# Attention's queries and keys projected token-major, in seven block products for eight, with the residual parked in DRAM

## The chip, the cores and the metric

One core of one Trainium2 chip runs the whole kernel. The metric is the device time in microseconds (us) of one execution. The profile and the trace are of one execution of the same program on the chip.

## The reference, cut to what matters

The program is a two-layer decoder trunk over 256 positions of width 2048, in float32. Layer 0 mixes by two recurrences, layer 1 by attention; each is followed by an MLP of width 8192. The change lies in layer 1's attention.

```python
qkv = (h @ w_qkv).astype(F32).reshape(bsz, seq, 3, ATTN_HEADS, HEAD_DIM)   # 16 heads of 128
q = partial_rope(qkv[:, :, 0], positions) * (HEAD_DIM ** -0.5)             # first 32 of 128 columns
k = partial_rope(qkv[:, :, 1], positions)
v = qkv[:, :, 2]
branches = [dilated_branch(q, k, v, w, d) for (w, d) in DILATED_GROUPS]    # (128,1) (512,4) (2048,16)
...                                                                        # merged by their softmax denominators
out = (num / den).reshape(bsz, seq, D_MODEL).astype(h.dtype)
return out @ w_o
```

`h` is `rms_norm(x, gain)`: the reciprocal root of each token's mean square multiplies whole rows, so it can be applied after a product with weights as well as before it.

## The kernel before, in words

**Number format.** Every float32 operand of a large product is split into a rounded part `hi` and a rest `lo`; a product is three TensorE products (hi*hi, hi*lo, lo*hi). Weights arrive as "units", tiles of 128x2048, one 1 MB DMA each on SP's queue, in one fixed order (the list `units`, filled ahead of the program). `unit()` hands out the next one and lets `fetch()` prepare the one that is two or three further on. `Weights.split` makes `hi` on ScalarE (L104) and `lo` on VectorE (L105); three buffers each for raw, hi and lo.

**Two ways to project.** *Feature-major* (`project`, with `cross`): a block of 128 output columns is the stationary operand's width, the 256 tokens stream; one unit is one block of 128 columns over all 16 blocks of the contraction, by 16 matmuls of 512 columns (hi of the weights against hi and lo of the tokens side by side) and 16 of 256 columns (lo of the weights). The result has features on partitions. *Token-major in pairs* (`blocks`): 8 units are 1024 output columns. Their first eight contraction blocks (the order `PAIRED`) are cut into 2 x 2 x 2 sub-blocks (even and odd contraction blocks, two halves of the tokens `j`, two groups of 512 columns `n`), and seven block products, three of them of sums of weights and sums of tokens (`formx`), replace eight; the other eight contraction blocks are plain. The steps of a pair stand in `ORDERS`: for `w_qkv` and `w2` it is a, t1, n7, t2, c, n6, t3, d, n2, t4, n3, where each of the seven letters is one product of 12 matmuls of 512 columns and each "n" is two (one for each half of the tokens, 24 matmuls). That makes 15 x 12 = 180 matmuls of 512 columns. The sums of weights `s` are made on VectorE (L132) and by accumulating DMAs on POOL's queue (L144, L150). Sums are picked out of PSUM part-way through ("events") and at the end ("final").

**Order on TensorE.** The matmuls of projections (`mm`, L183) and the transposes of the residual and of the MLP's hidden rows (`turn`, L186) are chained in the order of the program. All other TensorE instructions (scores, softmax transposes, mixes) are placed among them by the planner of the tile framework, from its own estimate of when their inputs are ready. Each engine then runs its list strictly in order.

**From MLP 0 to attention.** `second` adds MLP 0's output to the residual `xres` (L755), squares each finished 512 columns for the norm (L293), and `done(n)` queues `to_features(n)` in `later`, which turns the new residual to features, scaled by the norm's gain, and splits it into `bufa` and, for half of the columns, `formx`. The column groups finish in the order 1, 0, 3, 2. The normalizer itself (`rstd`: L297, L298, L319 to L324, on 128x2 values) needs all of the squares. `over_tokens` (L309) turns it into a row over tokens on TensorE and L848 copies it to `rs`.

**Attention before.** The first eight heads' values come from a pair (`values(0)`), whose events scale each bank by `rt`, the normalizer per token, into the tile `vg`. Then `rotary` (L819 to L842) makes the tables of cosines and sines, over 32 features and 256 tokens. Then for each head `scores` projects one unit for q and one for k feature-major, scales them by `rs` (L423 to L425), applies rope on the first 32 partitions (L853 to L856, a shuffle and three products), makes 128x384 scores in float32 (L866, L867), the softmax (L869 to L877), its transposes (L880, L882), and `mix` (L888, L889) multiplies with the values. Four heads run ahead of the second value pair (`values(32)`); the last four come after it. The output projection (`w_o`) starts directly behind; it takes the heads' groups of four in the order 0, 1, 2, 3, so it needs the last heads with its fourth unit, and adds the result to `xres` (L613).

Of the kernel before, what the change touches and what calls it, by code (L numbers as in the profile page):

```python
# [10 lines left out]
F32 = mybir.dt.float32  # L11
F32R = mybir.dt.float32r
BF16 = mybir.dt.bfloat16
I32 = mybir.dt.int32
# [6 lines left out]
P = 128  # L21
# [15 lines left out]
TC_ID, TC_LNC, TC_FREQ, TC_SIGN = 0, 128, 512, 513  # L37
NTAB = 514
# [3 lines left out]
def trunk_kernel(ctx, tc, x, xtok, cols, tab, masks, pos, fin, w_in, w_gate, w_out, w_qkv, w_o, w1, w2, out):  # L42
# [169 lines left out]
    def cross(p, w, jobs, parts="hl"):  # L212
        for part in parts:
            for blk, mov, first, last in jobs:
                h, l = w.part(blk * P, P)
                if part == "h":
                    mm(p, h, mov, start=first, stop=False, skip_group_check=True)
                else:
                    mm(p[:, S:], l, mov[:, :S], start=False, stop=last, skip_group_check=True)

# [7 lines left out]

    HA, XA, YA = direct, direct, direct
# [123 lines left out]
    def project(src, i, mov, acc=None):  # L353
        w = unit(src, i)
        p = pmm.tile([P, 512], F32, name="p")
        jobs = [(k, mov[:, k], k == 0, k == KB - 1) for k in range(KB)]
        if later:
            cross(p, w, jobs[:8], "h")
            flush()
            cross(p, w, jobs[8:12], "h")  # L360
            cross(p, w, jobs[:12], "l")
            jobs = jobs[12:]
        (acc or cross)(p, w, jobs)
# [53 lines left out]
    def scaled(p, z, acc=None):  # L417
        with urgent():
            if acc is direct:
                V.tensor_tensor(z, p[:, :S], rs, OP.mult)  # L420
            else:
                t = wk.tile([P, S], F32, name="t1", bufs=2)
                A.copy(t, p[:, S:])  # L423
                V.tensor_tensor(z, p[:, :S], t, OP.add)
                V.tensor_tensor(z, z, rs, OP.mult)  # L425

    def normed(p, name, bufs=2, acc=None):
        z = wk.tile([P, S], F32, name=name, bufs=bufs)
        scaled(p, z, acc)
# [14 lines left out]
    def hgrn(hd, vg):  # L444
# [4 lines left out]
        p = project(w_in, u0, bufa, HA)  # L449
        z = normed(p, "hz", 4, HA)  # L450
        lut(qp, z, AF.Sigmoid)
        V.scalar_tensor_tensor(qp, z, oml, qp, op0=OP.mult, op1=OP.mult)
        p = project(w_in, u0 + 1, bufa, HA)
        z = normed(p, "hz", 4, HA)
# [62 lines left out]
        p = project(w_in, u0 + 2, bufa, HA)  # L517
        z = normed(p, "hz", 4, HA)
# [8 lines left out]
    def lru_in(b):  # L527
        p = project(w_in, b, bufa, XA)
        xp = wk.tile([P, S + 4], F32, name="xp", bufs=1)
        V.memset(xp[:, :4], 0.0)  # L530
        scaled(p, xp[:, 4:], XA)
# [31 lines left out]
    def lru_out(b):  # L563
        p = project(w_in, 8 + b, bufa, YA)
        y = tmp.tile([P, S], F32, name="z")
        scaled(p, y, YA)
# [83 lines left out]
    nrm = out_project(w_out, "nmlp0", (2, 3, 0, 1))  # L650

    def blocks(src, i0, n0, mov, forms, events, final):
# [21 lines left out]
        for what, u in ORDERS[src is not w1]:  # L674
# [9 lines left out]
            for j in (1, 0) if n else (0, 1):  # L684
# [89 lines left out]
    def mlp(layer, nrm, nxt, gname):  # L774
# [33 lines left out]
    nx1 = Norm()  # L808
    mlp(0, nrm, nx1, "nmix1")
    pairs.close()  # L810

    vgs = mixers.enter_context(tc.tile_pool(name="vgs1", bufs=1))
    wk = mixers.enter_context(tc.tile_pool(name="wk2", bufs=2))
    angles = {}
    swap = [(i + 16) % 32 for i in range(32)]

    def rotary():
        ppi = wk.tile([32, S], I32, name="ra", bufs=2)
        nc.gpsimd.dma_start(ppi, bass.AP(tensor=pos.tensor, offset=pos.offset, ap=[[0, 32], [1, S]]))  # L819
        ang = wk.tile([32, S], F32, name="rb", bufs=2)  # L820
        cosT = wk.tile([32, S], F32, name="cosT", bufs=1)
# [258 lines left out]
```

## Time and profile before

| what | value |
|---|---|
| time, median of 3 runs | 2199.63 us (2199.01 to 2199.83) |
| span of the profiled execution, first to last instruction | 2197.5 us |
| outside the span (2199.63 - 2197.5) | 2.1 us |
| TensorE busy | 2149.2 us, 98% |
| VectorE busy | 1813.8 us, 83% |
| ScalarE busy | 1275.0 us, 58% |
| mean granted TensorE clock | 0.994 |
| values' first pair starts / output projection starts | 1127.73 us / 1416.26 us |

The profiled execution carries no stopwatch of its own beside its span; the times come from other executions of the same program, and its span lies 2.1 us below their median. In a row of the trace the mean is that of one instruction from start to end, which overlaps its neighbours on a pipelined engine; the distance from one start to the next is what an instruction costs its engine. Square brackets in the timeline hold the idle time ahead of an instruction and what ended it.

### The profile page before, as it was taken

The page shows a single profiled execution, that of the slowest core. Times are in us where ns is not written, and L with a number is a line of the kernel's source. Part 1 is how long each engine was busy: PE and PEld are TensorE (multiplying, and loading weights), DVE is VectorE, ACT ScalarE, POOL GpSimd, SP SyncE. Part 2 cuts the span into 40 slices and gives each one's busy share as a digit, 9 for nine tenths or more (in the row PEclk, how much of TensorE's full clock was granted, in tenths as well). Part 3 has the DMA queues.
Part 4 walks back from the last instruction along what each step waited for, and adds up shares of the span by engine and source line. Part 5 has one row for each costly group of instructions (what it writes and reads, how often), then busy time and mean ns, then how long its engine had stood idle before and what let it go on. Part 6 is the DMA issues. An engine that isn't in the chain of part 4 may idle for free.

```text
span 2197.5 us, 27706 instructions
## 1 busy us (share of the span) xinstructions
PE 2149.2 (98%) x11020; PEld 1833.2 (83%) x11020; DVE 1813.8 (83%) x2097; ACT 1275.0 (58%) x1427; POOL 48.2 (2%) x61
## 2 busy tenths in 40 slices
PE   9999999999999999999969999999999999999997
PEld 8999998878888888888758888888888888888886
DVE  8766787689879879889967887867998898898897
ACT  7444485566566566466645445455755755655664
POOL 0000000000000000000000000000000000000000
PEclk9999999999999999999989999999999999999999
DMA  8444446676787777777656456457777777777873
GB/s 314 156 166 160 154 154 211 186 250 226 228 254 235 230 236 245 227 240 248 202 152 211 155 192 209 165 175 217 231 224 239 245 230 233 259 219 227 268 233 131
DMA packets 66432, 468.86 MB, mean 213 GB/s; under 512 B 7408, under 2 KB 8176, under 8 KB 10368
## 3 DMA queue, kind: packets, MB, share of 16 engines
q1 hardware_dynamic: 58176, 410.89, 52.3%
q0 software_dynamic: 7840, 55.61, 13.6%
q8 instruction: 86, 1.41, 0.2%
q10 hardware_dynamic: 288, 0.61, 0.1%
q14 instruction: 42, 0.34, 0.0%
HBM read 464.98 MB, written 2.10 MB: 213 GB/s over the span
## 4 chain that ended last, share of the span: by engine, by line
PE 88%; ACT 6%; DVE 4%; issue 2%; DMA 1%; SPq 0%; DVEq 0%; ACTq 0%
PE p L183 61%; PE po L183 11%; PE pd L183 10%; ACT hi L104 3%; DVE lo L105 2%; PE pl L186 2%; PE pt L183 2%; PE pl L478 1%; DMA raw<-in_w 0%; ACT y L724 0%; ACT formh L595 0%; ACT y L720 0%; ACT y L725 0%; PE pl L867 0%; DVE xall L755 0%
## 5 line engine op out<-in xcount | busy, mean ns | idle before, releaser
L104 ACT CAST hi<-raw 128x2048 fp32r<-128x2048 f32 (+2 forms) x468 | 683.8, 1484 | 566.2 <-PE p L183 382.7
L105 DVE TENSOR_TENSOR lo<-raw,hi 128x2048 fp32r<-128x2048 f32 (+2 forms) x468 | 816.1, 1759 | 214.9 <-ACT hi L104 199.7
L183 PE MATMUL p<-hi,bufb 128*128 128x512 f32 x1408 | 449.3, 391 | 3.3 <-DVE xall L755 2.7
L183 PE MATMUL p<-hi,bufa 128*128 128x512 f32 x1136 | 366.5, 391 | 12.7 <-ACT y L720 7.9
L183 PE MATMUL p<-bufa,hi 128*128 128x256 f32 (+1 forms) x1792 | 365.5, 317 | 0.1
L183 PEld LDWEIGHTS p<-hi,bufb 128*128 128x128 f32 x1408 | 264.2, 188 | 61.7 <-DVE xall L755 6.2
L183 PEld LDWEIGHTS p<-bufa,hi 128*128 128x128 f32 x1792 | 294.4, 190 | 18.7 <-DVE hz L420 0.3
L183 PE MATMUL p<-lo,bufb 128*128 128x512 f32 x704 | 274.4, 390 | 1.5 <-DVE lo L105 1.5
L183 PEld LDWEIGHTS p<-hi,bufa 128*128 128x128 f32 x1136 | 213.2, 188 | 61.7 <-ACT y L720 11.3
L105 DVE TENSOR_TENSOR lo<-s,hi 128x2048 fp32r<-128x2048 f32 x102 | 233.2, 2287 | 33.6 <-ACT hi L104 31.6
L183 PE MATMUL p<-bufa,lo 128*128 128x256 f32 x1152 | 256.3, 287 | 0.0
L104 ACT CAST hi<-s 128x2048 fp32r<-128x2048 f32 x102 | 195.1, 1912 | 53.8 <-PE po L183 23.9
L183 PE MATMUL p<-lo,bufa 128*128 128x512 f32 x568 | 221.7, 390 | 1.9 <-DVE lo L105 1.9
L183 PEld LDWEIGHTS p<-bufa,lo 128*128 128x128 f32 x1152 | 189.6, 191 | 2.6
L183 PEld LDWEIGHTS p<-lo,bufb 128*128 128x128 f32 x704 | 132.2, 188 | 28.9 <-DVE lo L105 2.0
L183 PEld LDWEIGHTS p<-lo,bufa 128*128 128x128 f32 x568 | 106.7, 188 | 24.8 <-DVE lo L105 3.2
L132 DVE TENSOR_TENSOR s<-s,raw 128x2048 f32<-128x2048 f32 x50 | 114.1, 2282 | 3.1 <-DMA raw<-in_w 3.1
L183 PE MATMUL p<-hi,formx 128*128 128x512 f32 x288 | 95.3, 391 | 0.0
L105 DVE TENSOR_TENSOR lo<-t,hi 128x2048 fp32r<-128x2048 f32 x34 | 77.8, 2287 | 14.8 <-ACT hi L104 14.8
L183 PE MATMUL pd<-hi,bufa 128*128 128x512 f32 x256 | 84.8, 392 | 0.0
L183 PE MATMUL po<-hi,bufa 128*128 128x512 f32 x256 | 84.8, 392 | 0.0
L183 PE MATMUL po<-hi,bufb 128*128 128x512 f32 x256 | 84.2, 394 | 0.0
(297 smaller groups left out, 2894.7 us busy)
## 6 DMA issues: line engine op xcount, KB each, us to landing
raw<-in_w SPq DMA_DIRECT2D x224, 1024.0 KB, 5.1
raw<-in_w_in SPq DMA_DIRECT2D x46, 1024.0 KB, 4.9
raw<-in_w_qkv SPq DMA_DIRECT2D x46, 1024.0 KB, 4.9
t<-in_w SPq DMA_DIRECT2D x32, 1024.0 KB, 5.1
t<-in_w POOLq DMA_DIRECT2D x32, 1024.0 KB, 9.0
raw<-in_w_out SPq DMA_DIRECT2D x16, 1024.0 KB, 4.9
s<-in_w POOLq DMA_DIRECT2D x16, 1024.0 KB, 9.1
raw<-in_w_o SPq DMA_DIRECT2D x16, 1024.0 KB, 4.9
```

The lines of the kernel that those rows point to most:

```text
L104: A.copy(h, w)
L105: V.tensor_tensor(l, w, h.bitcast(F32), OP.subtract)
L132: V.tensor_tensor(held[to], held[x], held[y], OP.add)
L183: chain[:] = [after(T.matmul(*args, **kw), chain)]
L186: chain[:] = [after(T.transpose(out_, in_, ident), chain)]
L478: T.matmul(pl[:, j], kq[:, js], halves(qp[:, js], c, True), start=True, stop=True)
```

## The change

Queries and keys are projected token-major like the values: four pairs "q", each with 512 columns of queries (n = 0) and 512 of keys (n = 1) of four heads, and two pairs "v" of values, in the order `ATTENTION = "qvqqvq"`. The results are written over the residual: queries and keys into its first 1024 columns, values into its last 1024. The residual is stored to a DRAM tile `kept` as MLP 0 finishes it, on POOL's queue, and loaded back, on the same queue, ahead of the output projection's adds. Rope works along the free dimension on 128 tokens x 4 heads x 16 columns, six VectorE instructions for each half of the tokens and each of q and k; its tables are over tokens (128 x 2 x 16) and are made ahead of MLP 0. Each head's finished 128 tokens are turned to features by a TensorE transpose (64 in all, 4 to a group), placed by the planner. The row `rs` over tokens and its transposes go. In the first pair, two of the four sums are kept unscaled and scaled later, so that its first steps don't read the normalizer. In a `w_qkv` pair's plain steps the second half of the tokens now always goes first. `project` keeps only its other, direct form, for layer 0, where it was in use already. Mixes are delayed until their values exist. Cut to the core:

```diff
-            for v, heads in ((0, 24), (32, 8)):
-                plan2(w_qkv, v)
-                units.extend((w_qkv, v + 8 + i) for i in range(heads))
+            for i in range(6):
+                plan2(w_qkv, 8 * i)
...
-            for j in (1, 0) if n else (0, 1):
+            for j in (1, 0) if n or src is w_qkv else (0, 1):
...
                     to_features(n, gname, formx if n < 2 else None)
+                    at = slice(n * 512, n * 512 + 512)
+                    nc.gpsimd.dma_start(kept[:, :, at], xres[:, :, at])
...
+    kept = ctx.enter_context(tc.tile_pool(name="spill", bufs=1, space=bass.MemoryType.DRAM)).tile(
+        [P, 2, D], F32, name="kept")
+    rotary()
+    nx1 = Norm()
+    mlp(0, nrm, nx1, "nmix1")
+    pairs.close()
...
     rt = rstd(nx1)
-    rs = tmp.tile([P, S], F32, name="nr", bufs=1)
-    A.copy(rs, over_tokens(rt))
...
+    def token_pair(i, c0, ready, raw=()):
+        out_ = lambda n, j: xres[:, j, c0 + 512 * n:c0 + 512 * n + 512]
+        def put(n, j, r=rt):
+            def event(bank):
+                with urgent():
+                    if (n, j) in raw:
+                        A.copy(out_(n, j), bank)
+                    else:
+                        A.activation(out_(n, j), bank, AF.Copy, scale=r[:, j:j + 1])
+            return event
+        def add(n, j, bank, r=rt):
+            o = out_(n, j)
+            with urgent():
+                if (n, j) in raw:
+                    V.tensor_tensor(o, o, bank, OP.add if r is rt else OP.subtract)
+                else:
+                    V.scalar_tensor_tensor(o, bank, r[:, j:j + 1], o, op0=OP.mult, op1=OP.add)
+        def whole(n, j):
+            if (n, j) in raw:
+                with urgent():
+                    A.activation(out_(n, j), out_(n, j), AF.Copy, scale=rt[:, j:j + 1])
+            ready(n, j, out_(n, j))
+        def final(n, j, bank):
+            if (n, j) == (0, 1):
+                put(n, j)(bank)
+            else:
+                add(n, j, bank)
+            if (n, j) != (1, 1):
+                whole(n, j)
+        def u3(bank):
+            add(1, 1, bank, rtn)
+            whole(1, 1)
+        blocks(w_qkv, 8 * i, 0, bufa, formx,
+               {"a": put(0, 0), "t1": put(1, 1), "t2": put(1, 0, rtn), "t3": u3}, final)
+    def queries_keys(i, raw=()):
+        turned = [wk.tile([P, 4, S], F32, name="qT", bufs=2), wk.tile([P, 4, S], F32, name="kT", bufs=2)]
+        def ready(n, j, o):
+            t = o.rearrange("p (h c) -> p h c", h=4)
+            r = t[:, :, :32].rearrange("p h (two c) -> p h two c", two=2)
+            per = lambda a: a[:, j][:, None, :].to_broadcast([P, 4, 16])
+            with urgent():
+                b = wk.tile([P, 4, 2, 16], F32, name="rb", bufs=2)
+                V.tensor_tensor(b[:, :, 0], r[:, :, 1], per(sinT), OP.mult)
+                V.tensor_tensor(b[:, :, 1], r[:, :, 0], per(sinT), OP.mult)
+                for two in range(2):
+                    V.tensor_tensor(r[:, :, two], r[:, :, two], per(cosT), OP.mult)
+                    V.tensor_tensor(r[:, :, two], r[:, :, two], b[:, :, two], OP.add if two else OP.subtract)
+                p = psc.tile([P, 4, P], F32, name="pl", bufs=2)
+                for h in range(4):
+                    T.transpose(p[:, h], t[:, h], ident)
+                A.copy(turned[n][:, :, j * P:j * P + P], p)
+        token_pair(i, 0, ready, raw)
+        return turned
...
-    vg = values(0)
-    rotary()
-    for hd in range(8):
-        mix(hd, scores(8 + 2 * hd), vg)
-    pend = [scores(24 + 2 * i) for i in range(4)]
-    vg = values(32)
-    for i, bank in enumerate((("po", 1), ("pd", 1), ("pl", 2), ("pl", 2))):
-        mix(8 + i, pend[i], vg, *bank)
-    for i in range(4):
-        mix(12 + i, scores(40 + 2 * i), vg)
+    waiting, hd = [], 0
+    for i, what in enumerate(ATTENTION):
+        if what == "v":
+            token_pair(i, D // 2, lambda *_: None)
+        else:
+            q, k = queries_keys(i, ((0, 0), (1, 1)) if not i else ())
+            for h in range(4):
+                waiting.append((hd, scores(q[:, h], k[:, h])))
+                hd += 1
+                if i and ATTENTION[:i].count("v") * 8 >= hd:
+                    mix(*waiting.pop(0))
+        if what == "v":
+            while waiting:
+                mix(*waiting.pop(0))
+    for n in range(4):
+        cs = slice(n * 512, n * 512 + 512)
+        nc.gpsimd.dma_start(xres[:, :, cs], kept[:, :, cs])
```

More of the change, by code (lines that the diff above doesn't have):

```diff
@@ L210, in lut @@
         luts["now"].append(after(i, luts["now"][:1] or luts["before"]))
[L212 to L219, printed above, removed]
     def direct(p, w, jobs):
@@ L351, in tokens_group, with project @@
         return v
-    def project(src, i, mov, acc=None):
+    def project(src, i, mov):
         w = unit(src, i)
         p = pmm.tile([P, 512], F32, name="p")
[L356 to L363, printed above, removed]
+        direct(p, w, [(k, mov[:, k], k == 0, k == KB - 1) for k in range(KB)])
         return p
@@ L865, in scores @@
+    def scores(q, k):
         ps_ = psc.tile([P, 384], F32, name="pl", bufs=2)
```

125 lines of the change are left out of this document (44 added, 81 removed).

## The prediction

> **What bounds the kernel now.** I read the page first, then TensorE's waits, then busy time by stages.
>
> ```profile
> span 2197.5 us, 27706 instructions
> PE 2149.2 (98%) x11020; PEld 1833.2 (83%) x11020; DVE 1813.8 (83%) x2097; ACT 1275.0 (58%) x1427; POOL 48.2 (2%) x61
> 713.00:882.00 169.00, 168.00 (x757) 138.81 (x756) 147.57 (x99) 102.16 (x80) 5.21 (x6) 1.00 0.76 238
> 1194.00:1297.00 103.00, 103.00 (x607) 91.19 (x606) 91.02 (x204) 53.14 (x98) 0.00 (x0) 1.00 0.50 169
> PE pt L309 <- DVE nr L324: 10.2, 1, 10.2
> PE p L183 <- ACT y L720: 7.9, 8, 1.0
> PE p L183 <- DVE bufa L238: 4.2, 3, 1.4
> ```
>
> TensorE is busy 98% of the span, 48 us short of it. In the stretch of eight heads from 1194 it is busy in every microsecond (103.00 of 103), though VectorE is busy 91.02, 88%. In four MLP pairs (713 to 882), whose shape the attention takes over, it is idle 1.00 us of 169. So a change here is worth what it takes from TensorE's list of instructions, plus the long waits. The longest is L309 waiting 10.2 us for the normalizer, at the door of the attention. 0.2% (4.4 us) is about what a measurement of this kernel can tell from no change.
>
> **The products.** The timeline of TensorE in the first feature-major units, then lines of the chain of work that ended last.
>
> ```profile
> 1173.63 3.79 PE L183 MATMUL p<-bufa,hi 128*128 128x512 f32 x16
> 1177.26 2.08 PE L183 MATMUL p<-bufa,lo 128*128 128x256 f32 x16
> 1179.17 3.82 PE L183 MATMUL p<-bufa,hi 128*128 128x512 f32 x16
> 1182.83 2.08 PE L183 MATMUL p<-bufa,lo 128*128 128x256 f32 x16
> 1184.74 3.82 PE L183 MATMUL p<-bufa,hi 128*128 128x512 f32 x16
> ...
> 1079.84 8.16 PE p L183 x36
> 1141.25 0.87 PE pl L186 x8
> 1220.79 7.22 PE p L183 x45
> 1233.55 6.51 PE p L183 x40
> ```
>
> In the chain's lines the columns are start, length, what. A unit is 16 matmuls of 512 columns and 16 of 256; from 1179.17 to 1184.74 it takes 5.57 us. Eight units, four heads' queries and keys, take 44.56 us. The pair that replaces them is 180 matmuls of 512 columns; 36 take 8.16 us, one 0.2267, all 40.8. That is 3.76 us less a pair, and four pairs give **-15.0 us**. One head's period is 12.76 us (1220.79 to 1233.55): two units (11.14) and 1.62 of scores, softmax transposes and mix, which stay.
>
> **The head transposes.** 64 new ones. Eight transposes of 128x128 in float32 took 0.87 us in a row, 0.109 each: **+7.0 us**, all on TensorE's path. By a rule of the Trainium skill (TensorE: Matmul & The Clock Gate, Part 4: PE-mode transpose) a transpose costs about 275 ns in a kernel's context; the estimate by that page is 17.6 us for the 64, and the sum would be 10.6 us worse; the row of eight in 0.87 us speaks against it, since a start-to-end time is no distance between starts.
>
> **The start.** TensorE at the end of MLP 0 and the beginning of attention:
>
> ```profile
> 1115.23 0.39 PE L183 MATMUL po<-hi,bufb 128*128 128x512 f32 x1
> 1125.85 0.69 PE L309 MATMUL pt<-tab__181,nr 128*128 128x128 f32 x2 [10.23 <-DVE nr L324]
> 1127.73 0.79 PE L183 MATMUL pt<-hi,bufa 128*128 128x512 f32 x1 [1.19 <-ACT nr L848]
> 1141.09 1.03 PE L186 MATMUL pl<-tab__181,xall 128*128 128x128 f32 x8
> 1150.16 0.73 PE L183 MATMUL p<-hi,bufa 128*128 128x512 f32 x2 [1.45 <-DVE bufa L238]
> ```
>
> MLP 0's last matmul starts at 1115.23, the next could start at 1115.46. What comes instead is 10.23 us of waiting for the normalizer's chain, its two transposes, 1.19 us for the copy of `rs`, and then matmuls at a lowered clock. The products a, t1 and n7 (48 matmuls) end at 1141.09, 25.63 us later; at 0.2267 they need 10.88. The rest, 14.75 us, goes if a can follow at once: no instruction of the new list needs `rs`, the first two sums are kept unscaled, and the normalizer is first read after t2, 13.6 us (60 matmuls) later. Who is late next? The weights:
>
> ```profile
> 1115.66 1.90 ACT L104 CAST hi<-raw 128x2048 fp32r<-128x2048 f32 x1 [3.04 <-PE po L183]
> 1100.85 2.29 DVE L105 TENSOR_TENSOR lo<-raw,hi 128x2048 fp32r<-128x2048 f32 x1 [0.19 <-ACT hi L104]
> 1112.13 2.29 DVE L105 TENSOR_TENSOR lo<-s,hi 128x2048 fp32r<-128x2048 f32 x1 [2.46 <-ACT hi L104]
> 1115.61 2.28 DVE L132 TENSOR_TENSOR s<-s,raw 128x2048 f32<-128x2048 f32 x1
> 1118.47 0.27 DVE L823 CAST rb<-ra 32x256 f32<-32x256 int32 x1
> 1118.67 2.27 DVE L105 TENSOR_TENSOR lo<-raw,hi 128x2048 fp32r<-128x2048 f32 x1
> ```
>
> The lo of a is started at 1100.85 and that of t1 at 1112.13, 2.29 us each: both ready by 1115.46. The hi of n7 starts at 1115.66 (its buffer came free with MLP 0's last product), its lo at 1118.67, behind the sum L132 and a residual add, and ends 1120.9; new n7 would be due at 1115.46 + 5.44 = 1120.90. So it is just in time, with nothing to spare. Rotary's 18 or so instructions, which begin at 1118.47 between these splits, are gone from this place; ahead of MLP 0 they are cheaper (64 columns' width at most, for 256) and lie under products. At n6, which needs the group of features that is finished last, there was a wait of 1.45 us at 1150.16; it can stay or grow, as everything ahead of it moves up. I take **-14.75 us, and +2 us** for late weights and features (0 to 5). If the cover fails altogether, the third rival prices it.
>
> **Between pairs.** Six pairs now follow one another on one bank `pt`. The four MLP pairs idle 0.25 us each: +1.5 us for six. Below: nothing, as in the values' pair before. Above: 1.0 us each, the longest wait for ScalarE's evictions (L720), 6 us. The second half of the tokens going first leaves 12 matmuls (2.72 us) for `final`'s copy. **+1.5 us.**
>
> **VectorE.** Groups of its instructions in the attention before, and two rows for small shapes:
>
> ```profile
> L105 DVE TENSOR_TENSOR lo<-raw,hi 128x1024 fp32r<-128x1024 f32 x70 | 82.7, 1221 | 27.8 <-ACT hi L104 14.2 <-PE p L183 12.7 <-issue 0.4
> L105 DVE TENSOR_TENSOR lo<-raw,hi 128x2048 fp32r<-128x2048 f32 x12 | 27.5, 2290 | 7.5 <-ACT hi L104 7.1 <-ACT pT L882 0.4
> L425 DVE TENSOR_TENSOR hz<-hz,nr 128x256 f32<-128x256 f32 x32 | 13.4, 419 | 0.5
> L854 DVE TENSOR_TENSOR rb<-hz,cosT 32x256 f32<-32x256 f32 x31 | 12.3, 398 | 0.0
> L906 DVE SCALAR_TENSOR_TENSOR vg<-p,nr,vg 128x512 f32<-128x512 f32 x6 | 4.5, 746 | 1.7 <-PE p L183 1.7
> ...
> 1108.42 0.28 DVE L599 TENSOR_TENSOR y<-y 128x128 f32<-128x128 f32 x1
> 1121.13 0.14 DVE L297 TENSOR_REDUCE nm<-ss 128x2 f32<-128x8 f32 x1
> ```
>
> Feature-major, a head costs it four half-splits of 1.22 us and twelve instructions of 0.40 to 0.42 (two units x L424, L425, and rope's four): 4.9 + 4.9 = 9.8 us, or 0.77 of the period of 12.76. In the pair it does 11 splits and two sums of weights at 2.29 (the third sum is an accumulating DMA), four adds of 0.75, and rope's 24 instructions on 64 columns. These have no row: between 0.14 (128x2) and 0.28 (128x128). I take 0.21, half-way, as 64 lies between. That is 29.8 + 3.0 + 5.0 = 37.8 for four heads, 9.45 a head. The new period is (40.8 + 1.75 of transposes) / 4 + 1.62 = 12.26 us; 9.45 is 0.77 of it. The softmax stays. So VectorE is as loaded as before, under which TensorE lost nothing in the stretch from 1194: nothing added (0 to 8). ScalarE at 58% has room.
>
> **The tail.** Before, one head was left when the output projection started; now four are. The old tail, on TensorE and VectorE:
>
> ```profile
> 1416.26 0.40 PE L183 MATMUL p<-hi,bufb 128*128 128x512 f32 x1
> 1421.16 0.41 DVE L856 TENSOR_TENSOR hz<-ra,rb 32x256 f32<-32x256 f32 x1
> 1425.96 0.38 PE L866 MATMUL pl<-hz 128*128 128x128 f32 x2
> 1433.46 0.27 PE L880 MATMUL pd<-tab__181,as 128*128 128x128 f32 x1
> 1438.07 0.50 PE L183 MATMUL p<-hi,bufb 128*128 128x512 f32 x1 [0.46 <-ACT bufb L234]
> ```
>
> The projection starts at 1416.26. The last head's rope ends at about 1421.6, but its scores are placed at 1425.96 and its softmax transposes at 1433.46, both later than their inputs; the fourth unit's first matmul on the last heads then waits 0.46 us at 1438.07. So 21.8 us passed for one head, with hardly any slack. New, TensorE has three units (16.3 us) and four heads' 1.62 and transposes, 23.2 us, before it needs the last head. That head comes behind three others, at about 2.5 us of VectorE each (1.5 for its softmax, which is 88% of 12.76 less the 9.8; 1 for its share of four units' splits): 21.8 + 7.5 = 29.3 us at the old spacing, which is 6 us late; at the speed of the inputs alone about 8 us earlier (4.4 + 4.0 of late placing), and not late. I take **+5 us**, nearer to the spacing seen, range 0 to 14 (a long wait is followed by matmuls at the lowered clock, as at the start). The loads back from `kept` wait for the last head transposes and mixes on POOL's queue, where nothing else is queued until MLP 1. They are due first at the add behind the fourth unit, some 20 us after their own turn.
>
> **The spill.** 2 MB out and 2 MB back, issued by POOL. Behind a store on that queue stand the accumulating DMAs of the next pairs, and the store waits only for adds that are done. The SP stream loses a few us of bandwidth where the next weights are already in. 0 (0 to 2, as stalls).
>
> **Sum.** -15.0 + 7.0 - 14.75 + 2 + 1.5 + 5 = -14.25 us. 2197.5 - 14.25 = 2183.25 us of span, and with the 2.1 us outside, **2185.4 us**. Without any of the stalls taken, and with the 1.45 us of n6 saved too, it is 24.2 us: 2175.4.
>
> **Rivals.**
> *TensorE stuck on its own list (slower).* The head transposes stand in TensorE's strict list, where the planner puts them, behind rope on VectorE. If they stand too early, every one of 16 groups holds all matmuls behind it until a split (2.29), the add (0.75) and six rope instructions are through: up to 4.3 us, 69 us in all. From 1.2 us a group the kernel is slower by over 4.4 us ((14.25 + 4.4) / 16); at 2 us it is 2185.4 + 32 = 2217 us. Against it: in the tail above scores and transposes stand 4 us later than their inputs, and none of their lines is among the waits of TensorE. 0.08.
> *VectorE binds.* If rope's instructions cost 0.28, a head costs it 0.42 more; at its 88% that stretches the period by 0.48, 7.6 us for 16 heads: 2193. For it: 88% is all there is to see. Against: the moved load comes out even. 0.10.
> *The start doesn't move.* Something else that ends as late (the lo of n7, the last features) holds a or n7 for the same time; then the 14.75 come back and the 2 go: 2198.2 us. Against: the rows of a and t1. 0.14.
> *The transposes cost TensorE their whole length,* 0.27 each instead of 0.109, as if none overlapped its neighbour: 10.5 us more, 2195.9. Against: the eight in 0.87 us. 0.05. The page named above would have it about so.
>
> **How the numbers follow.** The forecast has 0.63, and its own range is 2175 to 2192. The range goes from 2174 to 2198: from no stall at all to the tail and pairs at their upper ends (+13.5 us), which takes in the second and fourth rival and about the start that doesn't move; slower cases and mishaps together are left out. Faster by over 4.4 us (below 2195.2): the forecast nearly whole (0.61), most of the second rival (0.08) and, where the start moves in part, a third of the third (0.05): 0.74. Same: the rest of the third, the fourth, and a little of the others: 0.15. Slower: the first rival and bad ends of the others: 0.11.
>
> **What would show it.** The first product of attention follows MLP 0's last without the 10 us gap, at full clock; L309 is gone there. A pair without heads' work takes 40.8 us. Groups of four transposes on `pl` take 0.44 us and wait for nothing. VectorE's share between the pairs is near 88%. A wait of some us stands at the fourth unit of `w_o`. I am wrong if TensorE's waits show the new transposes, or VectorE's lo, with more than a few us, or if the gap at the start stays.

## The result, and the profile after

The changed kernel takes 2188.88 us (median of 4, 2187.37 to 2190.48) beside 2199.73 us for the kernel before on the same chip: a ratio of 0.9948, 95% interval 0.9934 to 0.9962, or 10.85 us less. The forecast was 14.2 us less and a range of 2174 to 2198. A second set on another chip gave 2191.73 us, ratio 0.9958 (0.9944 to 0.9971).

The profiled execution is the one of 2187.37 us, the fastest of the four. From its page, the head:

```profile
span 2185.4 us, 27134 instructions
...
PE 2142.0 (98%) x10778; PEld 1814.9 (83%) x10778; DVE 1808.3 (83%) x1972; ACT 1301.5 (60%) x1408; POOL 60.1 (3%) x77
```

The stretch from the first product of attention to the output projection (columns: length; busy time and count of TensorE, its weight loads, VectorE, ScalarE, GpSimd; granted clock; share of the DMA engines; GB/s):

```profile
1116.20:1397.50 281.30, 276.89 (x1289) 229.33 (x1288) 232.15 (x302) 173.03 (x191) 11.57 (x14) 1.00 0.73 228
```

The span is 12.1 us shorter. TensorE is busy 276.89 of 281.30 us there; VectorE 232.15, 82.5%. TensorE's waits in the whole span (total, times, longest), some rows left out:

```profile
PE p L182 <- ACT y L697: 7.9, 8, 1.0
...
PE p L182 <- DVE lo L104: 4.9, 7, 1.2
PE p L182 <- DVE bufa L226: 3.6, 3, 1.4
...
PE pl L891 <- ACT qT L884: 2.0, 1, 2.0
PE p L182 <- ACT bufb L222: 1.9, 3, 1.4
...
PE po L913 <- ACT pT L907: 0.9, 1, 0.9
PE po L913 <- DVE bufb L223: 0.8, 1, 0.8
```

The wait for the normalizer (10.2 us) is gone, and no row of the whole list names the new transposes (L883) as the one that waits. New are the scores waiting for the turned queries (L891, 2.0 us in one piece) and the tail's mixes (L913, and matmuls waiting for `bufb`).

TensorE at the start, and one group of head transposes:

```profile
1115.98 0.39 PE L182 MATMUL po<-hi,bufb 128*128 128x512 f32 x1
1116.21 0.39 PE L182 MATMUL pt<-hi,bufa 128*128 128x512 f32 x1
...
1127.10 1.04 PE L185 MATMUL pl<-tab__181,xall 128*128 128x128 f32 x8
...
1135.59 0.73 PE L182 MATMUL p<-hi,bufa 128*128 128x512 f32 x2 [0.87 <-DVE bufa L226]
...
1145.48 0.60 PE L883 MATMUL pl<-tab__181,xall 128*128 128x128 f32 x4
1145.84 0.48 PE L182 MATMUL pt<-hi,bufa 128*128 128x512 f32 x1
1146.15 0.39 PE L182 MATMUL pt<-lo,bufa 128*128 128x512 f32 x1
1146.39 0.62 PE L182 MATMUL pt<-hi,bufa 128*128 128x512 f32 x2
```

MLP 0's last matmul starts at 1115.98 and the first product of attention at 1116.21, with no gap and at full clock: a, t1 and n7 end at 1127.10, 10.89 us for 48 matmuls. Four head transposes (L883) take 0.36 us (1145.48 to 1145.84), and the matmul behind them 0.31 instead of 0.23.

### The profile page after: what moved, and what is told of

Same layout as the page of the kernel before. It is cut to its first block, busy times and chain, and to the rows that moved or that the text cites. A ratio compares the mean times of both kernels' runs of the same rounds, so it can differ in the third digit from the quotient of the medians.

```text
span 2185.4 us, 27134 instructions
## 1 busy us (share of the span) xinstructions
PE 2142.0 (98%) x10778; PEld 1814.9 (83%) x10778; DVE 1808.3 (83%) x1972; ACT 1301.5 (60%) x1408; POOL 60.1 (3%) x77
## 4 chain that ended last, share of the span: by engine, by line
PE 86%; ACT 6%; DVE 4%; issue 2%; DMA 1%; SPq 0%; DVEq 0%; ACTq 0%
PE p L182 57%; PE po L182 11%; PE pd L182 10%; PE pt L182 4%; ACT hi L103 4%; DVE lo L104 2%; PE pl L185 2%; PE pl L453 1%; DMA raw<-in_w 0%; ACT y L701 0%; DMA raw<-in_w_qkv 0%; ACT formh L570 0%; ACT y L697 0%; ACT y L702 0%; PE pl L892 0%
## 5 line engine op out<-in xcount | busy, mean ns | idle before, releaser
L182 PE MATMUL p<-hi,bufa 128*128 128x512 f32 x1360 | 439.6, 391 | 12.2 <-ACT y L697 7.9
L182 PEld LDWEIGHTS p<-hi,bufa 128*128 128x128 f32 x1360 | 254.9, 188 | 69.7 <-ACT y L697 11.3
L104 DVE TENSOR_TENSOR lo<-s,hi 128x2048 fp32r<-128x2048 f32 x114 | 260.8, 2288 | 28.2 <-ACT hi L103 25.9
L182 PE MATMUL p<-lo,bufa 128*128 128x512 f32 x680 | 266.5, 392 | 3.8 <-DVE lo L104 3.7
L103 ACT CAST hi<-s 128x2048 fp32r<-128x2048 f32 x114 | 218.1, 1913 | 57.4 <-PE po L182 24.0
L182 PE MATMUL p<-bufa,hi 128*128 128x256 f32 x1280 | 240.9, 287 | 0.1
L182 PEld LDWEIGHTS p<-bufa,hi 128*128 128x128 f32 x1280 | 200.7, 191 | 0.4 <-DVE hz L400 0.3
L182 PE MATMUL p<-bufa,lo 128*128 128x256 f32 x640 | 182.7, 285 | 0.0
L182 PEld LDWEIGHTS p<-bufa,lo 128*128 128x128 f32 x640 | 122.4, 191 | 0.0
L131 DVE TENSOR_TENSOR s<-raw,t 128x2048 f32<-128x2048 f32 x38 | 86.9, 2286 | 0.0
```

The source lines that it names most:

```text
L103: A.copy(h, w)
L104: V.tensor_tensor(l, w, h.bitcast(F32), OP.subtract)
L131: V.tensor_tensor(held[to], held[x], held[y], OP.add)
L182: chain[:] = [after(T.matmul(*args, **kw), chain)]
```

## The experiments

Twelve runs were made (eleven kernels and the changed one again), each beside the kernel before on the same chip. Theory A, formed from the two traces: all of the gain is the start's; what seven products for eight save is spent again on head transposes, on dearer switches and on waits. Theory B is the prediction's split (12.75 us from the start, 1.5 us from all the rest). Theory C: the start gains only because nothing in the first pair needs the normalizer early.

### The start taken apart

**The row moved alone** (the kernel before):

```diff
     rs = tmp.tile([P, S], F32, name="nr", bufs=1)
-    A.copy(rs, over_tokens(rt))
...
     vg = values(0)
+    A.copy(rs, over_tokens(rt))
     rotary()
```

> The kernel before, with one thing of the change alone: the row over tokens (two transposes and a copy, L309 and L848) is made behind the first pair of values and no longer ahead of it; all else, feature-major queries and keys included, stays. Theory A (the gain is the start's; the pairs of queries and keys come out even, because what their fewer product columns save goes to head transposes, to dearer switches between instruction kinds and to idle time): the 10.2 us gap and the lowered clock behind it go, 12 to 15 us less than before, about 2186 us, as good as the changed kernel. Theory B (the prediction's split: the start gives about 12.75 us, the pairs 8 us less 6.5 us of waits and tail): also about 2187. Theory C (the start gains only because nothing in the first pair reads the normalizer early; here the first sum is scaled by it): the wait moves to t2, which needs the first bank back, and at least 5 us of the 14.75 stay, 2190 us or more.

2196.22 us, ratio 0.9984 (0.9975 to 0.9992): 4 us, not 14. Rows of TensorE, VectorE and ScalarE:

```profile
1133.01 0.80 PE L183 MATMUL p<-hi,bufa 128*128 128x512 f32 x1 [9.14 <-ACT vg L900]
...
1118.74 2.27 DVE L105 TENSOR_TENSOR lo<-raw,hi 128x2048 fp32r<-128x2048 f32 x1
...
1121.21 2.27 DVE L105 TENSOR_TENSOR lo<-s,hi 128x2048 fp32r<-128x2048 f32 x1
...
1123.68 2.27 DVE L105 TENSOR_TENSOR lo<-raw,hi 128x2048 fp32r<-128x2048 f32 x1
...
1130.03 0.16 DVE L324 SCALAR_TENSOR_TENSOR nr<-rs,nr 128x2 f32<-128x2 f32 x1
...
1129.80 1.28 ACT L207 ACT_TABLE_LOAD   x1 [6.68 <-DVE cosT L838]
...
1132.29 0.66 ACT L900 ACTIVATE vg<-p,nr 128x512 f32<-128x512 f32 x1
```

The first products now run, but the second half of n7 adds into the bank of t1, which ScalarE has yet to copy with the normalizer's scale (1132.29). On VectorE three splits of weights, 2.3 us each, and rotary's small instructions stand ahead of or among the normalizer's chain, which ends at 1130.2; then the sine's table is loaded ahead of the copies on ScalarE. TensorE waits 9.14 us. Theory C holds, with a wait at n7, not t2.

**All sums scaled at once** (the changed kernel):

```diff
-            q, k = queries_keys(i, ((0, 0), (1, 1)) if not i else ())
+            q, k = queries_keys(i)
```

> The changed kernel, with all sums of the first pair scaled at once by the normalizer (none kept unscaled). Theory A and B: the normalizer is ready at about 1122 us and the bank of the first product is needed again only at t2, at 1127 us in the changed kernel's trace, so TensorE waits for nothing new: within 1 us of the changed kernel, about 2188. Theory C: TensorE waits for ScalarE's scaled copy ahead of t2 or ahead of n7's second half; 3 us or more slower, 2191 or more.

2197.26 us, ratio 0.9987 (0.9978 to 0.9996), 6 to 8 us worse than the changed kernel in its two sets (2191.73 and 2188.88). Its row on TensorE:

```profile
1129.55 0.80 PE L182 MATMUL p<-hi,bufa 128*128 128x512 f32 x1 [5.21 <-ACT xall L835]
```

My expectation, a normalizer ready at about 1122 us, was wrong. Its chain on VectorE stands behind two splits and around a third and ends at 1128.2; in the changed kernel it ends no earlier (1128.8), but nothing there reads it before t2's sum. From a to the end of n7 this run takes 18.04 us, the changed kernel 10.89: the two unscaled sums carry 7 us of the start. Why the planner places the chain so late no run shows.

**The row put back** (the changed kernel; nothing reads it):

```diff
     rt = rstd(nx1)
+    rs = tmp.tile([P, S], F32, name="nr", bufs=1)
+    A.copy(rs, over_tokens(rt))
```

> The changed kernel with the row over tokens made where it was before (two transposes on TensorE ahead of the first product, and a copy), though nothing reads it: the pairs of queries and keys without the start's gain. Theory A: TensorE waits again for the normalizer ahead of the first product, 12 to 15 us come back, 2201 us, equal to the kernel before or up to 3 us slower: the pairs alone gain nothing. Theory B (pairs gain 8 us less 6.5): 2198, and if the tail and the waits are cheaper than predicted down to 2194. If the planner now puts the two transposes behind the first products: no change, 2189.

2201.16 us, ratio 1.0003 (0.9994 to 1.0011): no different from the kernel before. TensorE's wait:

```profile
PE pt L297 <- DVE nr L312: 7.7, 1, 7.7
```

With the wait at the door restored, nothing of the gain is left. (It is 7.7 us for 10.2: without rotary's instructions between its own, the normalizer's chain takes 2.5 us for 4.7.) The pairs of queries and keys, as placed here, gain nothing by themselves.

**The start alone** (the kernel before, with the row moved as above and):

```diff
-                    A.activation(v[:, j, n], bank, AF.Copy, scale=r[:, j:j + 1])
+                    if (n, j) in raw:
+                        A.copy(v[:, j, n], bank)
+                    else:
+                        A.activation(v[:, j, n], bank, AF.Copy, scale=r[:, j:j + 1])
...
-    vg = values(0)
+    vg = values(0, ((0, 0), (1, 1)))
```

> The kernel before with the whole of the start's cure and nothing else: the row over tokens behind the first pair of values, and the first and the last of that pair's four sums kept unscaled until they are complete. Queries and keys stay feature-major, the residual stays in place. Theory A (all of the gain is the start's): the wait of 9.1 us seen with the row moved alone goes too, the first products follow MLP 0 at full clock, 13 to 15 us less than before, about 2186 us: as fast as the changed kernel or up to 3 us faster. Theory B (the pairs of queries and keys hold a part of the gain): 2190 us or more, slower than the changed kernel. Theory D (rotary, still at this place, delays the splits of the weights, so that TensorE waits for lo instead): 2192 or more, with the wait named in the trace.

2188.41 us (2187.90 to 2188.92), ratio 0.9946 (0.9933 to 0.9958), with feature-major queries and keys: below the changed kernel, which gave 2191.73 (2189.64 to 2192.41) in the same set. One wait is left there:

```profile
PE pt L183 <- ACT vg L903: 2.6, 1, 2.6
```

**And rotary ahead of MLP 0** (the kernel of the run before, with `rotary()` moved and its scratch shared):

```diff
+    rotary()
     nx1 = Norm()
     mlp(0, nrm, nx1, "nmix1")
...
     A.copy(rs, over_tokens(rt))
-    rotary()
```

> The start alone, with rotary's tables made ahead of MLP 0, as the changed kernel has it (two of them kept, one scratch tile shared); queries and keys stay feature-major and the residual in place. In the start alone without this, TensorE waited 2.6 us at t2 for ScalarE's copy of the first sum, which stood behind the sine on ScalarE's queue. Theory A: that wait goes, and 2 to 3 us with it: 2186 us, 2185 to 2187, faster than the changed kernel. Rival: the copy was late for another reason (ScalarE's casts); no change, 2188.

2185.01 us, ratio 0.9929 (0.9917 to 0.9942). That wait is gone, and TensorE is busy nearly throughout:

```profile
1120.00:1400.00 280.00, 279.12 (x1523) 242.06 (x1522) 234.09 (x433) 146.45 (x220) 2.60 (x3) 1.00 0.59 194
```

So the start is worth 15.7 us (2200.67 to 2185.01). Against this the rest of the change costs 4 us by its first set (0.9948; the intervals overlap) and 6 us by its second (0.9958; they don't). Theory A is right about the place of the gain, and too kind to the pairs.

### What the pairs pay for

**No head transposes** (the copies take the tokens as they lie, so the scores are of other numbers):

```diff
-                p = psc.tile([P, 4, P], F32, name="pl", bufs=2)
-                for h in range(4):
-                    T.transpose(p[:, h], t[:, h], ident)
-                A.copy(turned[n][:, :, j * P:j * P + P], p)
+                A.copy(turned[n][:, :, j * P:j * P + P], t)
```

> The changed kernel without its 64 head transposes: the finished tokens are copied as they lie into the tiles of turned heads, so the scores are of other numbers; the copies stay. By the changed kernel's trace a group of four takes 0.36 us and makes the next matmul 0.12 us later: 16 x 0.48 = 7.65 us less, plus what TensorE waited for right behind them (0.34 and part of 2.03 us): theory A 2180 us. By the prediction's price (0.109 each) 7.0 us less: 2182. If a transpose cost its whole 0.27 us: 17 us less, 2171.

2183.16 us, ratio 0.9930 (0.9916 to 0.9943); the profiled span is 5.0 us below the changed kernel's. That is less than the 7.5 us that the transposes take in the changed kernel's trace; a part came back as waits for VectorE, 7.7 us where they were 4.9, the longest 2.7:

```profile
PE p L182 <- DVE lo L104: 7.7, 6, 2.7
```

Behind the longest (1168.10) the granted clock is 0.50 for 3.4 us, which costs 1.7 us more. So the transposes had been covering late splits. A cost of 0.27 us each is excluded: it would be 17 us.

**No spill** (`kept` and its eight DMAs left out, so the residual of attention's output is what lies there):

```diff
-                    nc.gpsimd.dma_start(kept[:, :, at], xres[:, :, at])
...
-        nc.gpsimd.dma_start(xres[:, :, cs], kept[:, :, cs])
```

> The changed kernel without its eight DMAs to and from the DRAM tile: the residual of attention's output is then what lies in its place (queries, keys and values). It shows what the 4 MB cost. Prediction and theory A: 0 to 1 us less than the changed kernel, since no wait in its trace names these transfers. Rival: the loads and stores hold up the weights on the same DMA engines or the accumulating DMAs on the same queue (raw takes 6.6 us to land there instead of 4.9): 3 us or more less, 2185 us.

2190.99 us (2188.30 to 2191.63) beside the changed kernel's 2191.73 (2189.64 to 2192.41) in the same set: no cost that these runs can tell.

**The changed kernel again:**

> The changed kernel itself, so that the other three are compared with it on the same chip: 2188.9 us, 2187 to 2191.

2191.73 us, a little above what was expected, and its profiled execution (span 2189.6) differs from the first mainly in one respect. The same two stretches, first in the earlier execution, then in this one (granted clock third from the end):

```profile
1268.00:1280.00 12.00, 12.00 (x58) 10.02 (x57) 9.37 (x19) 7.85 (x17) 0.00 (x0) 1.00 0.69 249
1425.00:1440.00 15.00, 14.78 (x71) 12.03 (x70) 7.69 (x10) 7.08 (x12) 0.72 (x1) 1.00 0.38 115
```

```profile
1268.00:1280.00 12.00, 12.00 (x51) 9.85 (x50) 7.93 (x16) 6.63 (x12) 0.00 (x0) 0.87 0.59 217
1425.00:1440.00 15.00, 14.65 (x63) 11.54 (x64) 4.86 (x7) 5.25 (x11) 0.72 (x1) 0.90 0.21 60
```

TensorE in the second execution:

```profile
1264.00 0.60 PE L883 MATMUL pl<-tab__181,xall 128*128 128x128 f32 x4
1266.64 0.49 PE L891 MATMUL pl<-kT,qT 128*128 128x128 f32 x2 [2.04 <-ACT qT L884]
...
1267.62 0.98 PE L892 MATMUL pl<-kT,qT 128*128 128x256 f32 x2
1268.04 0.99 PE L182 MATMUL pt<-hi,formx 128*128 128x512 f32 x1
...
1269.25 1.05 PE L182 MATMUL pt<-hi,formx 128*128 128x512 f32 x2
```

Both executions have the wait of 2.03 or 2.04 us at L891. In the second the clock is halved right behind it for 3.4 us (0.87 on average over 12 us): the matmuls start 0.43 apart instead of 0.23 (1269.25 to 1270.53 holds three), which costs about 1.6 us beside the wait. The same happens in the tail (0.90 over 15 us; 1.4 us). That is 3.0 of the 4.2 us between the two spans; the other 1.2 us were there before the scores (1264.00 for 1262.81).

### The tail and the placing of the scores

In the changed kernel's trace the wait at L891 and the tail read so (TensorE, ScalarE and one rope instruction of VectorE; then the tail on TensorE):

```profile
1262.81 0.60 PE L883 MATMUL pl<-tab__181,xall 128*128 128x128 f32 x4
1265.44 0.49 PE L891 MATMUL pl<-kT,qT 128*128 128x128 f32 x2 [2.03 <-ACT qT L884]
...
1263.01 1.90 ACT L103 CAST hi<-raw 128x2048 fp32r<-128x2048 f32 x1 [2.96 <-PE p L182]
1264.81 0.58 ACT L884 COPY qT<-pl 128x512 f32<-128x512 f32 x1
...
1257.27 0.22 DVE L876 TENSOR_TENSOR rb<-xall,sinT 128x64 f32<-128x64 f32 x1
```

```profile
1416.21 0.70 PE L913 MATMUL po<-pT,xall 128*128 128x256 f32 x2 [0.86 <-ACT pT L907]
...
1419.16 0.67 PE L913 MATMUL po<-pT,xall 128*128 128x256 f32 x2 [0.83 <-DVE bufb L223]
...
1422.11 0.50 PE L182 MATMUL p<-hi,bufb 128*128 128x512 f32 x1 [1.43 <-ACT bufb L222]
```

The planner puts the last head transposes and the scores in one group, behind the next pair's n7. The copy between them (1264.81) stands on ScalarE behind a cast of 1.90 us, whose buffer comes free at the same moment. In the tail a mix waits for the copy of its turned softmax, the next for the split of the mix ahead of it, which has the one bank `po`, and the projection for the copies of the mixes' results.

**The values last:**

```diff
-ATTENTION = "qvqqvq"
+ATTENTION = "qvqqqv"
...
-        st = wk.tile([P, 384], F32, name="pT", bufs=5)
+        st = wk.tile([P, 384], F32, name="pT", bufs=9)
```

(and one buffer instead of two for each of the turned queries and keys)

> The changed kernel with the second pair of values last (order q v q q q v; nine buffers for the turned softmax, and one each for the turned queries and keys). The last heads' softmax then runs under a pair of products, and only eight mixes are left when the output projection starts. Theory A (the tail's waits of 3.6 us, 0.86 + 0.83 + 1.43 + 0.23 + 0.22, are VectorE's and ScalarE's latency behind the last q pair): they shrink to 1 us or less, 2186 us, if the eight mixes at the end do not wait for the eight splits of their results. Rival: the mixes run one after another through the one bank po (about 1 us each with its split), in the order of the heads, and hold the output projection's third unit: no gain or up to 4 us slower, 2189 to 2193.

2188.72 us (2188.48 to 2189.44), ratio 0.9947 (0.9935 to 0.9960), 3 us below the changed kernel in the same set, though the ratios' intervals overlap (0.9944 to 0.9971). Theory A expected the tail's waits to shrink to 1 us. They come to 3.7 us, as much as before, now for the one bank of the mixes, as the rival had it:

```profile
PE p L182 <- ACT bufb L222: 2.1, 5, 1.0
PE pl L891 <- ACT qT L884: 2.0, 1, 2.0
PE po L913 <- DVE bufb L223: 1.6, 2, 0.8
```

**The mixes in four banks, and scores issued later** (on top of the values last):

```diff
-            while waiting:
-                mix(*waiting.pop(0))
+            for m, bank in zip(range(len(waiting)), 2 * (("po", 1), ("pd", 1), ("pl", 2), ("pl", 2))):
+                mix(*waiting.pop(0), *(bank if i == 5 else ("po", 1)))
```

(and a pair's scores go to `later`, so they are issued behind the next n7)

> The changed kernel with the values' pair last, and with each pair's scores issued behind the first plain step (n7) of the next pair instead of right behind the head transposes; the eight mixes at the end go through four banks in turn. Theory E (in some executions the clock of TensorE is halved for 3.4 us behind two places where it ran small instructions and waited, the scores that wait 2.03 us for the copy of the turned queries and the tail; each costs 1.7 us beside the wait): both waits go, and the halvings with them. 2188.7 less 2.0, 1.7 and about 1.5 of mixes' waits: 2183.5 us, and the executions lie within 1 us of one another, where the changed kernel's lay within 5 us over its two sets. Rival: the planner puts the scores where they wait again, or the wait moves to VectorE's splits, which at 82% of this stretch have little slack: 2187 to 2189, with lo among TensorE's waits by 3 us or more above the 4.5 seen.

2182.99 us (2182.88 to 2183.70), ratio 0.9920 (0.9907 to 0.9934): the lowest time of all, below the kernel before and both sets of the changed one. The ratio's interval overlaps that of the start with rotary ahead of MLP 0 (0.9917 to 0.9942), but that kernel ran in the same set, and its five times (2184.65 to 2185.57) all lie above these, by 2.0 us in the median. Only half of the theory is borne out:

```profile
1403.40 0.59 PE L913 MATMUL po<-pT,xall 128*128 128x256 f32 x2
...
1404.05 0.60 PE L913 MATMUL pl<-pT,xall 128*128 128x256 f32 x2
...
1404.71 0.60 PE L913 MATMUL pd<-pT,xall 128*128 128x256 f32 x2
...
1405.36 0.60 PE L913 MATMUL pl<-pT,xall 128*128 128x256 f32 x2
```

The scores' wait in the same kernel:

```profile
PE pl L891 <- ACT qT L884: 2.0, 1, 2.0
```

The eight mixes now run in two groups of four, without a wait. The scores stand where they stood, and so do their wait and, in this execution, the halved clock behind it: the planner had put them behind n7 before, so that issuing them there moved nothing. The gain of 5.7 us over the values last (5.9 us between the two profiled spans) is the tail's: from the start of the output projection to the end of its first group of columns the two traces take 38.15 and 32.81 us.

**The scores held behind n7 by an explicit order** (on top of that):

```diff
-        T.matmul(ps_[:, :P], q[:, :P], k[:, :P], start=True, stop=True)
+        after(T.matmul(ps_[:, :P], q[:, :P], k[:, :P], start=True, stop=True), chain)
```

> The kernel with the values last and four banks for the mixes (scores issued later), with one line more: the first score matmul of each head may not stand on TensorE ahead of the next pair's first plain step, n7. In the kernel without that line the scores still stood right behind the head transposes, the wait of 2.04 us for the copy of the turned queries stayed, and the clock was halved for 3.4 us behind it in the profiled execution, which cost 1.7 us more. Theory E: both go, 3.7 us less, 2179.5 us (2181.3 if the halving was in the profile alone and not in most executions). Rival: the scores, 11 us later, push softmax and mixes into the next stages and a wait of 2 us or more appears at the mixes or at lo: 2183 or more.

2183.17 us (2181.91 to 2186.93), ratio 0.9929 (0.9915 to 0.9942): no change, for the same reason; the wait of 2.0 us is still in its trace. The clock stayed at 1.00 there this time.

**Held behind n6** (the same with one line changed):

```diff
-        later.append(work)
+        later.append(lambda: later.append(work))
```

> As the kernel with the scores held back, but behind the second plain step of the next pair (n6, three products and 8.2 us later). The wait of 2.04 us stood behind n7 in the trace already: there the planner puts the last head transposes and the scores in one group, and the copy between them stands on ScalarE behind a cast of 1.90 us whose buffer comes free at the same moment; so holding the scores until n7 changed nothing. Theory E: behind n6 the copy is long done; the wait goes, and the halved clock behind it, 2 to 3.7 us less than 2183.2: 2179.5 to 2181. Rival: the scores meet another late input there, or the softmax, 8 us later, makes the mixes or lo late by as much: 2183 or more.

2188.87 us, ratio 0.9950 (0.9936 to 0.9964): 6 us worse, as the rival had it, though by other waits than it named. The wait for the queries is gone, and two others are there:

```profile
1266.16 0.50 PE L182 MATMUL pt<-hi,formx 128*128 128x512 f32 x1 [2.62 <-ACT xall L835]
...
1319.43 0.50 PE L182 MATMUL pt<-hi,formx 128*128 128x512 f32 x1 [2.34 <-ACT xall L835]
```

The scores held back leave t2 waiting for its bank `pt`, whose copy into `xres` (L835) comes late. Why it does was not tried. That the earlier pair's queries, which it overwrites, have to be turned first is a candidate, not shown.

## Why the prediction was right, step by step

The median moved by 10.85 us where 14.25 were forecast, within the range and with the sign. The split was worse than the total. In the profiled spans, which differ by 12.1 us, the terms that came out dearer than forecast add up to some 6.5 us and the cheaper ones to 4.3: that the total came so close is in part luck.

The terms can be read from the two traces by adding up TensorE's starts, from t2 of the first pair (the eight transposes ahead of it included) to the end of the output projection's first group of columns: 1141.09 to 1447.33 before and 1127.10 to 1435.13 after, 306.2 and 308.0 us. A product matmul counts with the distance to the next start; one that stands right behind another kind of instruction counts 0.2267 us (0.1195 with 256 columns), and its delay counts with that kind. Idle time counts as a wait.

| step | predicted | measured |
|---|---|---|
| products, four pairs | -15.0 | -13.5: 276.8 before, 263.3 after |
| head transposes | +7.0 | +7.5, the delay of the matmul behind each group included |
| the heads' scores, softmax transposes and mixes | 0 | +1.6: 26.7 before, 28.3 after |
| start | -14.75 + 2 | -15.3: the gap whole, n6's wait 0.87 for 1.45; alone on the chip 15.7 |
| between pairs | +1.5 | +3.5: waits of 0.34, 0.12, 2.03 and 1.05 |
| tail | +5 | +3.2: 0.86 + 0.13 + 0.83 + 1.43 + 0.23 + 0.22, less 0.46 before |
| end of MLP 0 | 0 | +0.75 (1115.46 to 1116.21) |
| behind the stretch | 0 | +0.1 |

The 0.75 us at the end of MLP 0 is no cost of the change that can be told: in the executions without a wait ahead of a, a starts anywhere from 1115.47 to 1116.72, also with feature-major queries and keys.

**What bounds it, the start, the products:** right in kind. That a could follow MLP 0 at once, with n7's weights just in time, is what the trace shows; I allowed 2 us for late weights and it took less than nothing. What I did not see is how much hung on the two unscaled sums. I named them as the reason why the normalizer is needed late, and then, before the run that scales all sums at once, thought them dispensable; they carry 7 us. The products' saving was 1.5 us too large: I set a unit's price between the heads (5.57 us) against a matmul's price among MLP pairs (0.2267), where it averages 0.2286 in the attention (263.3 us for 1152).

**The step that was mis-sized** is the one on pairs and heads. I took 1.62 us for a head's small instructions as it was among matmuls of 256 columns and carried it over; by the sum above it is 1.67 before and 1.77 after. And I took a quarter of a microsecond for the seam between pairs from MLP pairs, which have no scores; the waits came to 3.5 us for 1.5. How much of the heads' 1.6 us is due to switches between kinds of instructions cannot be told from the starts, and no run separates it.

**The tail** was right in kind and place and 2 us too dear; the four banks show it by its removal (the values last alone did not remove it). The halving of the clock behind a wait, which I had only reckoned with there, comes behind the scores' wait too, and not in every execution; it is left out of the table, since the first profiled execution has none.

**VectorE:** rope's instructions on 64 columns last 0.22 us (I took 0.21), but the next starts 0.13 us later (1257.27 and 1257.40), so a length was counted as a cost; the share was 82.5%, not near 88%. The second rival fell; the run without head transposes, where the waits for splits grew to 7.7 us, shows that the reserve is small all the same.

**The rivals:** no new transpose waits long on TensorE, so the slower case did not come. The start did move. A head transpose does not cost 0.27 us: four took 0.36 us, and leaving all 64 out took 5.0 us off the span. The Trainium skill (TensorE: Matmul & The Clock Gate, Part 4: PE-mode transpose) has about 275 ns in a kernel's context; as a price per transpose the measurement decides against it here.

The larger lesson is in the start alone. The change is called after its seven products for eight, which I forecast at 8 us net of transposes; they gain nothing as placed (the row put back, ratio 1.0003), and a kernel with none of them has a lower time than the changed one (2185.01). With the tail's waits removed they gain a little: 2182.99 in the same set, 2.0 us less. The stretch summed above takes 305.9 us in the start with rotary ahead of MLP 0, 303.6 with the four banks, and in the changed kernel 308.0 or, with both halvings of the clock, 311.9.

## What to carry to other kernels

A change of several parts is best priced by the part that touches the longest wait: here two sums kept unscaled and a row moved gave as much as the whole change. Fewer product columns help only if what they need around them (turns, seams, the last group's latency) is smaller than they are; count the small instructions at the place where they will stand, not where they stood. A chain of tiny instructions that something waits for is late by whatever large instructions stand ahead of it on its engine; in the changed kernel the chain came no earlier, and the gain came from an order in which nothing needs it until later. A waste that comes in some executions and not in others, such as the halved clock here, has to be counted over several profiles before two kernels are compared by one each.

## What the runs showed of the hardware that was not expected

TensorE's granted clock fell to one half for 3.4 us behind a wait of only 2.04 us (second execution, 1266.64), and stayed at 1.00 behind the same wait in the first. The stretch without a product matmul was 4.0 us there (1264.00 to 1268.04): four transposes, the wait, and eight score matmuls. In the tail of the second execution the same was seen. Behind a wait of 1.45 us at n6 in the kernel before it did not fall.

It is no rare event: between the end of the first pair's n7 and the output projection, seven of the ten profiled executions with token-major queries and keys have it. Nor does it need the small matmuls: in the run without head transposes it comes behind a wait of 2.67 us between product matmuls (1168.10). Yet in the start alone a wait of 2.62 us (1142.98) left the clock at 1.00.

The clock records of the traces show what differs. In each of the fourteen profiled executions all changes of the clock lie whole multiples of 3.413 us apart, so they fall on a fixed grid of steps, which lies elsewhere in each execution. From full clock it fell at the end of every step in which TensorE was idle for 1.97 us or more, and of no step with 1.94 us or less, but for two in the tail with 1.89 us of idle time among small matmuls (the second execution and the run with all sums scaled). In the second execution all 2.04 us of the scores' wait lie in one step, in the first 1.94, and the 2.62 us of the start alone are cut in two, 1.86 the larger part. Between 1.89 and 1.97 us, whether transposes and score matmuls count as idle may decide; no run here separates that.

The Trainium skill (TensorE: Matmul & The Clock Gate, Part 1: The HAM clock gate) has the clock halve after about 3.4 us of idleness seen through a window of that length which runs free of the program, and its Part 4: PE-mode transpose says that transposes do not count as busy in the same way. The grid and its length agree with the free-running window; that some 2 us of idle time in one window are enough is what these traces show instead of 3.4.
